# Expert tokens as rows fetched from DRAM, a ring of fourteen weight tiles, and a pad ahead of the last stage's operands

## Chip, cores and metric

One core of one Trainium2 chip. Times are device microseconds (us) of one execution. The kernel is written with a scheduler of tiles: each engine has its own queue of instructions, and the queues meet at semaphores.

## What is computed

The reference runs two blocks over 512 tokens of width 1024. The first ends in a mixture of experts: of 32 experts in 4 groups each token takes the best group and the best two experts in it.

```python
def hierarchical_moe(hn, w_router_group, w_router_expert, w_gate, w_up, w_down):
...
    gates = g_w * jax.nn.softmax(top_v, axis=-1)
...
    xs = tokens[row_token].reshape(n_blocks, EXPERT_BLOCK, d)

    def run_block(args):
        xb, e = args
        return (jax.nn.silu(xb @ w_gate[e]) * (xb @ w_up[e])) @ w_down[e]
...
    out = jnp.zeros((n, d), jnp.float32).at[row_token].add(ys.astype(jnp.float32) * row_gate[:, None])
```

Ahead of it stands a state-space and convolution mixer; behind it a second block with windowed attention, an mLSTM, a merge of their branches and a convolutional feed-forward part. All is float32.

## The kernel before, in words

Tokens are kept as 4 tiles of 128 (NT = 4), the width as 8 tiles of 128 (KD = 8). The program has three stages. phase_a is the mixer, to about 450 us. phase_b has the router (`route`, to about 474 us) and the experts (`experts`, L781, to about 1000 us). phase_c is the second block. Most of its products, as of phase_a's, are at L227: a float32 product as three products of operands that are split in a high and a low part (hT_hi, hT_lo with wh, wl).

**Experts.** Each expert has 64 slots (NSLOT); what does not fit goes through `overflow` (L619), a branch on the count `nov`. The loop runs over 8 groups of 4 experts, each as 2 pairs, 16 pairs in all. For a group, `dispatch` (L743) builds a one-hot matrix S of 512 tokens by 256 slots on DVE, and `gather` (L728) multiplies it with the normalized tokens on PE: 64 matmuls of 128x256 (L738, tile pxg) give the slots' activations transposed, xg. `gather` is a generator; PE works it off piece by piece inside the pairs of the group before. The tokens are split in hn_hi and hn_lo by `route_split` (L441), on ACT, DVE and POOL. A pair has 64 matmuls for gate and up (pgu, L808), an activation, four transposes (phT, L723), and 32 matmuls for down (pyd, L834). `slot_gates` (L753) finds each slot's gate weight and its row in the result (pgs, L763). For the first seven groups (NVIA = 7) POOL scatters the pair's rows to the DRAM buffer y_rows by an indirect DMA (L842); the last group is combined by matmuls (pcomb, L879). `add_rows` (L859) reads y_rows back and adds it to x.

**Weights.** `load_w` (L161) loads tiles of 1 MB in turn into a ring of ten; almost all loads stand in SP's queue, in order, and each waits until the matmuls that read the tile's former content are done. A pair reads twelve tiles: four for gate, four for up, four for down. `expert_loads` (L403) gives their order, with the context products' weights (MK, MV) behind pairs 9 and 12. `prefetch` (L395) takes the next loads from it, `expert_w` one at a time; `phase_b` (L331) calls prefetch(10) once behind `route`, and once on POOL's queue ahead of the overflow's branch, since SP cannot issue loads while it waits at it. `add_rows` issues its eight transfers (L867) on SP's queue as well, between the weights of pairs 13 and 14.

**Places.** Pools are allocated from two sides of the on-chip memory. c_h is opened first in phase_c (L1464) on the right side and holds hT_hi and hT_lo; pools opened on that side later lie below it.

Of the kernel before, what the change touches and what calls it, by code (L numbers as in the profile page):

```python
# [15 lines left out]
I32 = mybir.dt.int32  # L16
# [108 lines left out]
class K:  # L125
# [35 lines left out]
    def load_w(self, src, nk=4, cols=512, rows=False, queue=None):  # L161
        if self.loaded:
            return self.loaded.popleft()
        pool, n = self.rings[self.ring_at % len(self.rings)]
        self.ring_at += 1
        w = pool.tile([P, nk, cols], F32, tag="w", name="w")
        (queue or self.nc.sync).dma_start(w, src if rows else src.rearrange("(k p) c -> p k c", p=P))
        return w
# [77 lines left out]
    def setup(self):  # L246
# [40 lines left out]
        self.ye = self.dram.tile([YROWS, D], F32, name="y_rows")  # L287
        self.mod_at = 0
# [42 lines left out]
    def phase_b(self):  # L331
# [6 lines left out]
        ws = [self.load_w(w[k * P:(k + 4) * P, AK:AK + 512]) for k in (0, 4)]  # L338
        self.route(bp, rt, ws)
        rt.release()  # L340
        wk = self.pool("b_wk", bufs=1)
        i = self.ring_at % 5
        turn = [p for p, _ in self.rings[i:] + self.rings[:i]]
        self.set_rings([(p, 1) for p in (ringm[1], ringm[1], *turn[:3], ringm[2], ringm[2], ringm[0], *turn[3:])])
        self.loads = self.expert_loads({9: MK, 12: MV})
        self.ahead = deque()
        self.prefetch(10)
# [47 lines left out]
    def prefetch(self, n, queue=None):  # L395
        self.ahead.extend(self.load_w(src, rows=True, queue=queue) for src in islice(self.loads, n))

    def expert_w(self):
        if not self.ahead:
# [27 lines left out]
    def route_alloc(self):  # L427
        self.hh = self.bcp.tile([P, NT, KD, P], F32R, tag="s16", name="hn_hi")
        self.hl = self.bcp.tile([P, NT, KD, P], F32R, tag="bcg", name="hn_lo")
# [11 lines left out]
    def route_split(self, t):  # L441

        nc = self.nc
        r = self.xss[:, 0, t:t + 1]
        x = self.x[:, t, :].rearrange("p (h q j) -> p h j q", h=2, j=4)
        h, l = (v[:, t].rearrange("p (h j) q -> p h j q", h=2) for v in (self.hh, self.hl))
        nc.scalar.activation(h, x, AF.Copy, scale=r)
        if t > 1:
            if t == 2:
                self.xr = self.wide.tile([P, 2, D], F32, tag="cva", name="xr")  # L450
            xr = self.xr[:, t - 2, :]
            nc.scalar.activation(xr, self.x[:, t, :], AF.Copy, scale=r)
# [32 lines left out]
    def route_steps(self):  # L485
# [4 lines left out]
        self.route_split(0)  # L490
# [4 lines left out]
        self.route_split(1)  # L495
# [8 lines left out]
    def route(self, bp, rt, ws):  # L504
# [71 lines left out]
        for i, s in enumerate((1, 2, 4, 8, 16)):  # L576
# [7 lines left out]
        self.nov = bp.tile([1, 1], I32, name="nov")  # L584
        nc.vector.tensor_copy(self.nov, src[0:1, E - 1:E])
# [26 lines left out]
        self.gshl = bp.tile([P, NT, E, 3], F32R, name="gshl")  # L612
        tok = self.cst[:, CS["token"]]
        nc.vector.scalar_tensor_tensor(self.gshl[:, :, :, 2], oh2f, float(T),
                                       tok[:, :, None].to_broadcast([P, NT, E]), op0=ALU.mult, op1=ALU.add)
        nc.vector.tensor_copy(self.gshl[:, :, :, 0], gs)
        nc.vector.tensor_sub(self.gshl[:, :, :, 1], gs, self.gshl[:, :, :, 0].bitcast(F32))

    def overflow(self, op, wk):  # L619
# [5 lines left out]
        ei = op.tile([1, 1], I32, name="ei")  # L625
        nov = nc.values_load(self.nov[0:1, 0:1], min_val=0, max_val=2 * T // S)
        with tc.If(nov > 0), tc.For_i(0, nov, 1) as b:
# [37 lines left out]
            for _ in self.gather(xg, Sm, S):  # L665
                pass
# [22 lines left out]
            y = op.tile([S, D], F32, name="oy")  # L689
# [38 lines left out]
    def gather(self, xg, S, n):  # L728

        nc = self.nc  # L730
        g = self.pv[:, PV["norm_ffn4"]]
        for q in range(KD // 2):
            px = self.aux.tile([P, 2, n], F32, tag="ax", name="pxg")
            for kk in range(2):
                k = 2 * q + kk
                for t in range(NT):
                    for j, h in enumerate((self.hh, self.hl)):
                        nc.tensor.matmul(px[:, kk, :], h[:, t, k, :], S[:, t, :],  # L738
                                         start=(t == 0 and j == 0), stop=(t == NT - 1 and j == 1))
            nc.vector.tensor_mul(xg[:, 2 * q:2 * q + 2, :], px, g[:, 2 * q:2 * q + 2, None].to_broadcast([P, 2, n]))  # L740
            yield

    def dispatch(self, S, xg, grp):  # L743
# [7 lines left out]
        return self.gather(xg, S, 4 * NSLOT)  # L751

    def slot_gates(self, wk, S, grp):  # L753

        nc = self.nc
        gs = wk.tile([P, 2], F32, tag="gs", name="gs", bufs=2)
        at = [wk.tile([P, 1], I32, tag=f"at{pr}", name="at", bufs=2) for pr in range(2)]
        for pr in range(2):
            sc = slice(pr * P, pr * P + P)
            pg = self.aux.tile([P, 6], F32, tag="ax", name="pgs")  # L760
            e0 = grp * 4 + pr * 2
            for t in range(NT):
                nc.tensor.matmul(pg, S[:, t, sc],  # L763
                                 self.gshl[:, t, e0:e0 + 2, :].rearrange("p e j -> p (e j)"),
                                 start=(t == 0), stop=(t == NT - 1))
            for i in range(2):
                r = slice(64 * i, 64 * i + 64)
                nc.vector.tensor_reduce(gs[r, pr:pr + 1], pg[r, 3 * i:3 * i + 2], op=ALU.add, axis=AX.X)
                nc.vector.tensor_scalar(at[pr][r, :], pg[r, 3 * i + 2:3 * i + 3], float(NOROW), None, op0=ALU.add)
# [11 lines left out]
    def experts(self, bp, wk, extra):  # L781
# [4 lines left out]
        Ss = [SS[:, i * D:i * D + D].rearrange("p (t c) -> p t c", t=NT) for i in range(2)]  # L786
        xgs = [self.wide.tile([P, KD, 4 * NSLOT], F32, tag=t, name="xg") for t in ("u", "cva")]
        for _ in self.dispatch(Ss[0], xgs[0], 0):
            pass
        back = self.keys  # L790
        for grp in range(8):
            S, xg = Ss[grp % 2], xgs[grp % 2]
            via = grp < NVIA
            if via:
                ahead = self.dispatch(Ss[1 - grp % 2], xgs[1 - grp % 2], grp + 1)
            for pr in range(2):
                e0 = grp * 4 + pr * 2
                pgu = []
                for _ in range(2):
# [16 lines left out]
                if pr == 0:  # L816
                    gs, at = self.slot_gates(wk, S, grp)
                    if not via:
                        ST = Ss[1 - grp % 2].rearrange("p t c -> p (t c)").rearrange("p (r c) -> p r c", r=2)
                        self.take_back(S, ST)  # L820
                        self.add_rows()
                if via:
                    for _ in islice(ahead, 2):
                        pass
# [20 lines left out]
                else:  # L845
                    yhl = self.wide.tile([P, 2, D], F32R, tag="u", name="yhl")
# [7 lines left out]
                if extra[1].get(2 * grp + pr):  # L854
                    extra[1][2 * grp + pr]()
        for _ in back:
            pass

    def add_rows(self):  # L859

        nc = self.nc
        for h, tag in enumerate(("s16", "bcg")):
            r = self.bcp.tile([P, 2, 2, D], F32, tag=tag, name="rows_back")
            for i in range(2):
                t = 2 * h + i
                for k in range(2):
                    nc.sync.dma_start(r[:, i, k, :], self.ye[T * k + P * t:T * k + P * t + P, :])  # L867
                for k in range(2):
                    nc.vector.tensor_add(self.x[:, t, :], self.x[:, t, :], r[:, i, k, :])
# [594 lines left out]
    def phase_c(self):  # L1464
# [5 lines left out]
        lo = ph.tile([P, KD, T], F32R, name="hT_lo")  # L1470
        pt = self.pool("c_tmp", bufs=2)
# [844 lines left out]
```

## Time and profile before

| what | us |
|---|---|
| median of 3 runs | 2036.63 (2034.98 to 2036.65) |
| the profiled execution | 2032.46 |
| its span on the core | 2030.7 |
| PE busy in the span | 1962.0 |
| DVE, ACT, POOL busy | 1027.2, 661.0, 114.1 |
| mean granted clock of PE | 0.993 |
| bytes moved by DMA | 392.86 MB |

The span goes from the first to the last instruction, and the execution's time has some 2 us around it. The clock is a share of full speed. A busy PE is not a PE at its peak: matmuls are pipelined, so a matmul's own duration is longer than the step from one start to the next.

### The profile page before, as it was taken

To read this page: it belongs to the slowest core of one execution; us is meant where nothing else is said; L and a number is where in the kernel's file an instruction comes from. 1 tells how busy PE (TensorE), PEld (TensorE's weight loads), DVE (VectorE), ACT (ScalarE), POOL (GpSimd) and SP (SyncE) were. 2 spreads that over 40 slices of the span, in tenths; PEclk is the share of its full clock that TensorE was granted. 3 is DMA by queue.
4 is the path that set the end of the run, shared out by engine and by line. 5 is a ranking of instruction groups with operands and counts; after the bars stand their busy time and mean duration, and the time that the engine had idled before them with its cause. 6 is when DMAs were issued, how large, how long until landed. Compare 5 with 4: busy or idle time off the path is not lost.

```text
span 2030.7 us, 24234 instructions
## 1 busy us (share of the span) xinstructions
PE 1962.0 (97%) x9533; PEld 1367.5 (67%) x9533; DVE 1027.2 (51%) x1958; ACT 661.0 (33%) x1139; POOL 114.1 (6%) x139
## 2 busy tenths in 40 slices
PE   5999999999999999998999999999999999999999
PEld 5777676785444433443377888778888788888887
DVE  3766758434224111102477687684734666656632
ACT  3332325331010000000256666422433354334411
POOL 2000002000000010000122010000000020000000
PEclk9999999999999999998999999999999999999999
DMA  7344355536999999999832222543133442323231
GB/s 285 129 163 143 112 204 189 181 136 251 420 403 375 421 418 394 422 364 387 343 111 68 63 71 73 173 120 110 58 111 125 135 145 83 104 84 103 96 114 50
DMA packets 121797, 392.86 MB, mean 193 GB/s; under 512 B 12436, under 2 KB 31540, under 8 KB 93008
## 3 DMA queue, kind: packets, MB, share of 16 engines
q1 hardware_dynamic: 110912, 353.63, 47.1%
q0 software_dynamic: 6848, 33.05, 4.1%
q10 hardware_dynamic: 3920, 4.59, 0.7%
q8 instruction: 76, 1.25, 0.3%
q14 instruction: 41, 0.34, 0.1%
HBM read 370.73 MB, written 24.17 MB: 194 GB/s over the span
## 4 chain that ended last, share of the span: by engine, by line
PE 74%; issue 15%; DVE 5%; DMA 4%; ACT 2%; POOL 1%; SPq 0%; POOLq 0%; ACTq 0%; DVEq 0%
PE mm L227 41%; PE pgu L808 10%; PE pyd L834 6%; PE pxg L738 3%; PE pck L1368 2%; DMA w<-in_w_down_dram 2%; PE pav L1737 2%; PE ppt L1724 1%; DMA w<-in_w_up_dram 1%; PE pn L1866 1%; PE pn L1867 1%; DVE wl L132 1%; PE psc L1691 1%; DMA cst<-in_cst_dram 1%; PE pst L1883 1%
## 5 line engine op out<-in xcount | busy, mean ns | idle before, releaser
L132 DVE TENSOR_TENSOR wl<-w,wh 128x1024 fp32r<-128x1024 f32 x206 | 251.5, 1222 | 357.4 <-ACT wh L131 352.3
L131 ACT ACTIVATE wh<-w 128x1024 fp32r<-128x1024 f32 x210 | 222.3, 1059 | 545.4 <-PE mm L227 500.5
L808 PE MATMUL pgu<-w,xg 128*64 128x512 f32 x1024 | 234.9, 597 | 6.0 <-DMA w<-in_w_up_dram 4.6
L227 PE MATMUL mm<-hT_hi,wl 128*128 128x512 f32 (+1 forms) x560 | 219.7, 392 | 0.0
L227 PE MATMUL mm<-hT_lo,wh 128*128 128x512 f32 (+1 forms) x560 | 218.7, 391 | 0.7 <-POOL hT_lo L1312 0.7
L227 PE MATMUL mm<-hT_hi,wh 128*128 128x512 f32 (+1 forms) x560 | 218.7, 391 | 0.0
L808 PEld LDWEIGHTS pgu<-w,xg 128*64 128x64 f32 x1024 | 75.0, 138 | 149.9 <-issue 139.7
L834 PE MATMUL pyd<-w,hT 128*64 128x512 f32 x512 | 143.0, 618 | 9.5 <-DMA w<-in_w_down_dram 7.1
L227 PE MATMUL mm<-hnT_hi,wh 128*128 128x512 f32 (+1 forms) x368 | 144.6, 394 | 0.9 <-DVE rv L137 0.6
L227 PE MATMUL mm<-hnT_lo,wh 128*128 128x512 f32 (+1 forms) x368 | 141.7, 385 | 0.0
L227 PE MATMUL mm<-hnT_hi,wl 128*128 128x512 f32 (+1 forms) x368 | 141.0, 386 | 0.2 <-POOL wl L132 0.2
L227 PEld LDWEIGHTS mm<-hT_lo,wh 128*128 128x128 f32 x560 | 105.3, 188 | 25.5 <-POOL hT_lo L1312 0.9
L227 PEld LDWEIGHTS mm<-hT_hi,wl 128*128 128x128 f32 x560 | 105.3, 188 | 22.9 <-issue 0.4
L227 PEld LDWEIGHTS mm<-hT_hi,wh 128*128 128x128 f32 x560 | 105.3, 188 | 22.2
L834 PEld LDWEIGHTS pyd<-w,hT 128*64 128x64 f32 x512 | 42.5, 140 | 83.4 <-issue 73.6
L227 PE MATMUL mm<-wh,hT_lo 128*128 128x512 f32 (+1 forms) x256 | 95.3, 372 | 1.0 <-DVE hT_lo L1308 1.0
L227 PE MATMUL mm<-wh,hT_hi 128*128 128x512 f32 (+1 forms) x256 | 95.2, 373 | 0.0
L227 PE MATMUL mm<-wl,hT_hi 128*128 128x512 f32 (+1 forms) x256 | 94.7, 372 | 0.0
L227 PEld LDWEIGHTS mm<-hnT_hi,wh 128*128 128x128 f32 x368 | 69.4, 189 | 27.0 <-issue 7.4
L227 PEld LDWEIGHTS mm<-hnT_hi,wl 128*128 128x128 f32 x368 | 69.5, 189 | 16.2 <-issue 1.5
L227 PEld LDWEIGHTS mm<-hnT_lo,wh 128*128 128x128 f32 x368 | 69.5, 189 | 14.3 <-issue 2.1
L714 DVE SCALAR_TENSOR_TENSOR esg<-eth,pgu 128x512 f32<-128x512 f32 x16 | 11.0, 685 | 126.4 <-ACT eth L712 126.4
(552 smaller groups left out, 3468.3 us busy)
## 6 DMA issues: line engine op xcount, KB each, us to landing
w<-in_w_up_dram SPq DMA_DIRECT2D x82, 1024.0 KB, 10.2
w<-in_w_down_dram SPq DMA_DIRECT2D x72, 1024.0 KB, 9.6
w<-in_w_gate_dram SPq DMA_DIRECT2D x60, 1024.0 KB, 7.9
w<-in_w_in_dram SPq DMA_DIRECT2D x56, 1024.0 KB, 6.6
w<-in_w_mod_dram SPq DMA_DIRECT2D x24, 1024.0 KB, 4.8
w<-in_w_out_dram SPq DMA_DIRECT2D x16, 1024.0 KB, 5.2
x_res<-in_x_dram SPq DMA_DIRECT2D x8, 512.0 KB, 8.5
y_rows<-zero_rows POOLq DMA_DIRECT2D x4, 1024.0 KB, 9.2
```

Of the source, the lines that this page charges most:

```text
L131: nc.scalar.activation(hi, src, AF.Copy)
L132: (eng or nc.vector).tensor_sub(lo, src, hi.bitcast(F32))
L227: nc.tensor.matmul(ps[i][:, a:b], x, y, start=st, stop=sp, skip_group_check=(per > 1 or halves))
L738: nc.tensor.matmul(px[:, kk, :], h[:, t, k, :], S[:, t, :], start=(t == 0 and j == 0), stop=(t == NT - 1 and j == 1))
L808: nc.tensor.matmul(ps[64 * i:64 * i + 64, :], xg[:, k, c:c + NSLOT], ws[i][k // 4][:, k % 4, :], start=(k == 0), stop=(k == KD - 1), skip_ ...
L834: nc.tensor.matmul(py[dh][64 * i:64 * i + 64, :], hT[:, f, 64 * i:64 * i + 64], ws[i][:, f % 2 * 2 + dh, :], start=(f == 0), stop=(f == 3) ...
L1368: nc.tensor.matmul(ps[t], self.hc[:, k, t * P:(t + 1) * P], ws[k // 4][:, k % 4, :], start=(k == 0), stop=(k == KD - 1))
L1691: nc.tensor.matmul(pl, u.qs[i], kst[0][:, kv, c0 * P:c0 * P + n], start=True, stop=False)
L1724: nc.tensor.transpose(pt[:, i, :], u.p[i][:, s * P:(s + 1) * P], self.ident)
L1737: nc.tensor.matmul(po[64 * x:64 * x + 64], v[:, vs, kv * 64:kv * 64 + 64], PT[s][:, 2 * x:2 * x + 2, :], start=(s == 0), stop=(s == nk - 1 ...
L1866: nc.tensor.matmul(pn, qs[:, j, cs], C, start=True, stop=False)
L1867: nc.tensor.matmul(pn, Pm[:, j, cs], mv[:, c, h, :], start=False, stop=True)
```

## The change

1. `route_split` is replaced by `route_rows`: ACT scales a tile of tokens and writes it as rows to a DRAM buffer h_rows. `gather` goes. `fetch` reads, by an indirect DMA on POOL, the row of each of a pair's 128 slots; `turn_rows` transposes them on PE (8 transposes of 128x128) into xg. For the offsets the slot matmul gets a fourth column, the token's number, and `slot_gates` becomes a part of `dispatch`. In the overflow's body the same takes the place of the gather.
2. The tiles that held hn_hi and hn_lo become four more weight tiles (ring_s, ring_bcg), and `prefetch(14)` comes ahead of `route`.
3. The read-back of y_rows becomes four loads of 1 MB in the ring, between gate and up of pair 15; `add_rows` only adds, one pair later.
4. A tile of 96 bytes a partition (pad_right) is allocated in c_h behind hT_lo.

```diff
+        more = [self.bcp.tile([P, 2, 4, 512], F32, tag=t, name="ring_" + t) for t in ("s16", "bcg")]
+        self.set_rings([(p, 1) for p in (ringm[1], ringm[1], *turn[:3], ringm[2], ringm[2], ringm[0], *turn[3:])])
+        self.rings[0:0] = [(r[:, i], 0) for r in more for i in range(2)]
+        self.loads = self.expert_loads({9: MK, 12: MV})
+        self.ahead, self.rows_back = deque(), []
+        self.prefetch(14)
         self.route(bp, rt, ws)
...
-            self.prefetch(10, nc.gpsimd)
+            self.prefetch(14, nc.gpsimd)
...
     def prefetch(self, n, queue=None):
-        self.ahead.extend(self.load_w(src, rows=True, queue=queue) for src in islice(self.loads, n))
+        for src in islice(self.loads, n):
+            if type(src) is int:
+
+                w = self.ring_tile().rearrange("p (k a) b -> p k (a b)", k=2)
+                self.nc.sync.dma_start(w, self.ye.rearrange("(k t p) d -> t p k d", k=2, t=NT)[src])
+                self.rows_back.append(w)
+            else:
+                self.ahead.append(self.load_w(src, rows=True, queue=queue))
...
+                if e0 == 30 and src is wu:
+                    yield from range(NT)
...
+    def route_rows(self, t):
+
+        h = self.hrow[:, t % 2, :]
+        self.nc.scalar.activation(h, self.x[:, t, :], AF.Copy, scale=self.xss[:, 0, t:t + 1])
+        self.nc.scalar.dma_start(self.hd[t * P:t * P + P, :], h)
...
+    def fetch(self, rows, at):
+
+        self.nc.gpsimd.indirect_dma_start(
+            out=rows, out_offset=None, in_=self.hd[:, :],
+            in_offset=bass.IndirectOffsetOnAxis(ap=at[:, 0:1], axis=0), bounds_check=T - 1, oob_is_err=False)
+
+    def turn_rows(self, xg, rows, hf, n):
...
+        px = self.aux.tile([P, 4, n], F32, tag="ax", name="pxg")
+        for j in range(4):
+            nc.tensor.transpose(px[:, j, :], src[:, hf, j, :], self.ident[:n, :n])
+        nc.vector.tensor_mul(xg, px, g.to_broadcast([P, 4, n]))
...
+        gs, at = self.dispatch(wk, S, 0)
+        for pr in range(2):
+            self.fetch(rows[:, pr, :], at[pr][:, 1:2])
+        for _ in islice(self.keys, 3):
             pass
+        turn(0)
...
                 if pr == 0:
...
+                    turn(1)
+                    if grp < 7:
+                        gs2, at2 = self.dispatch(wk, S, grp + 1)
+                        for i in range(2):
+                            self.fetch(rows[:, i, :], at2[i][:, 1:2])
+                    else:
                         self.take_back(S, ST)
-                        self.add_rows()
...
+                elif grp < 7:
+                    turn(0)
+                else:
+                    self.add_rows()
...
         lo = ph.tile([P, KD, T], F32R, name="hT_lo")
+        ph.tile([P, 24], F32, name="pad_right")
```

Three places show how the order moves. First SP's queue around the router, where the first loads for the experts stand (w, ring_s and ring_bcg are tiles of the ring; nov is the overflow's count). Before:

```order
L167 DMA w<-in_w_in_dram 128x4x512 x2
L167 DMA w<-in_w_gate_dram 128x2048 x2
L167 DMA w<-in_w_up_dram 128x2048 x2
L167 DMA w<-in_w_gate_dram 128x2048 x2
L167 DMA w<-in_w_up_dram 128x2048 x2
L167 DMA w<-in_w_down_dram 128x2048
L626 TENSOR_LOAD nov
```

Now:

```order
L165 DMA w<-in_w_in_dram 128x4x512 x2
L165 DMA w<-in_w_up_dram 128x2048
L165 DMA ring_bcg<-in_w_gate_dram 128x2048
L165 DMA ring_s_3271<-in_w_gate_dram 128x2048 x2
L165 DMA ring_bcg<-in_w_gate_dram 128x2048
L165 DMA w<-in_w_up_dram 128x2048
L165 DMA w<-in_w_down_dram 128x2048 x2
L165 DMA w<-in_w_up_dram 128x2048 x2
L165 DMA w<-in_w_down_dram 128x2048 x2
L165 DMA w<-in_w_gate_dram 128x2048 x2
L629 TENSOR_LOAD nov
```

Fourteen expert tiles stand ahead of the load of nov where nine stood, and the first gate tiles lie in the four new ones.

Second PE's queue behind the gate and up matmuls of a pair. Before:

```order
L808 MATMUL pgu<-w,xg 64x512 x23
L723 MATMUL phT<-cst,esg 128x128 x4
L738 MATMUL pxg<-SS,hn_hi 128x256
L738 MATMUL pxg<-SS,hn_lo 128x256
L738 MATMUL pxg<-SS,hn_hi 128x256
```

Now:

```order
L824 MATMUL pgu<-w,xg 64x512 x24
L733 MATMUL phT<-cst,esg 128x128 x4
L1438 MATMUL pml<-mr,rsel 128x4 x8
L751 MATMUL pxg<-cst,rows 128x128 x5
L853 MATMUL pyd_4450<-w,hT 64x512
L853 MATMUL pyd_4451<-w,hT 64x512
```

The one-hot products of the next group are gone from between the pair's own matmuls, and the transposes of the next pair's rows stand there.

Third SP's queue at the read-back of y_rows. Before:

```order
L167 DMA w<-in_w_gate_dram 128x2048 x4
L167 DMA w<-in_w_up_dram 128x2048 x4
L867 DMA rows_back<-y_rows 128x1024 x8
L167 DMA w<-in_w_down_dram 128x2048 x4
L167 DMA w<-in_w_gate_dram 128x2048 x4
```

Now:

```order
L165 DMA ring_bcg<-in_w_gate_dram 128x2048 x2
L165 DMA w<-in_w_gate_dram 128x2048 x2
L406 DMA w<-y_rows 128x2x1024 x4
L165 DMA w<-in_w_up_dram 128x2048 x4
L165 DMA ring_s_3271<-in_w_down_dram 128x2048 x2
L165 DMA ring_bcg<-in_w_down_dram 128x2048 x2
```

The read-back stood ahead of pair 14's down weights and stands ahead of pair 15's up weights, in four tiles of the ring.

## Rows read from the trace of the kernel before

**Rows 1.** The page: busy time of each engine (its line).

```profile
PE 1962.0 (97%) x9533; PEld 1367.5 (67%) x9533; DVE 1027.2 (51%) x1958; ACT 661.0 (33%) x1139; POOL 114.1 (6%) x139
```

**Rows 2.** Windows of 40 us across the expert stage, and the sum of its thirteen.

```profile
core 0: us, PE busy (x) PEld busy (x) DVE busy (x) ACT busy (x) POOL busy (x), PEclk, DMA share, GB/s
480.00:520.00 40.00, 39.89 (x194) 17.85 (x192) 8.85 (x26) 4.61 (x11) 3.20 (x3) 1.00 0.92 370
520.00:560.00 40.00, 38.91 (x198) 18.29 (x195) 8.77 (x22) 3.94 (x10) 0.99 (x1) 1.00 1.01 422
...
920.00:960.00 40.00, 31.78 (x140) 11.99 (x138) 13.16 (x20) 3.67 (x6) 0.97 (x1) 0.88 0.95 387
...
sum 520.00, PE 494.56 PEld 211.39 DVE 105.41 ACT 40.76 POOL 23.35; mean PE 38.04 PEld 16.26 DVE 8.11 ACT 3.13 POOL 1.80
```

**Rows 3.** The DMA view of 474:1000, its line of totals.

```profile
DMA packets 33046, 207.47 MB, mean 394 GB/s; under 512 B 4297, under 2 KB 4297, under 8 KB 9594
```

**Rows 4.** Window of everything behind the experts, columns as in rows 2.

```profile
1010.00:2031.00 1021.00, 1006.94 (x4963) 815.18 (x4961) 621.54 (x1174) 440.08 (x806) 60.02 (x83) 1.00 0.31 101
```

**Rows 5.** Timeline of PE in 1700:1703, operand hT: start, duration, instruction.

```profile
1699.80 0.40 PE L227 MATMUL mm<-hT_hi,wl 128*128 128x512 f32 x1
...
1702.84 0.39 PE L227 MATMUL mm<-hT_hi,wh 128*128 128x512 f32 x1
```

**Rows 6.** Timeline of PE in 1365:1368.2, operand attT.

```profile
1365.06 0.62 PE L227 MATMUL mm<-attT,wh 128*128 128x512 f32 x2
...
1367.78 0.62 PE L227 MATMUL mm<-attT,wh 128*128 128x512 f32 x2
```

**Rows 7.** Timeline of PE in 496:498.5: the gather.

```profile
496.10 0.36 PE L738 MATMUL pxg<-SS,hn_hi 128*128 128x256 f32 x1
...
498.44 0.28 PE L738 MATMUL pxg<-SS,hn_lo 128*128 128x256 f32 x1
```

**Rows 8.** Timeline of PE in 989:991: four 128x128 transposes.

```profile
989.15 0.74 PE L723 MATMUL phT<-cst,esg 128*128 128x128 f32 x4 [0.82 <-DVE esg L715]
```

**Rows 9.** Timeline of SP's queue in 405:490, weight loads: first issue, time to the last.

```profile
409.67 12.59 SPq L167 DMA_DIRECT2D w<-in_w_gate_dram  x2
...
448.40 4.31 SPq L167 DMA_DIRECT2D w<-in_w_up_dram  x2
466.37 15.50 SPq L167 DMA_DIRECT2D w<-in_w_down_dram  x4
```

**Rows 10.** Windows of 10 us around the first expert, columns as in rows 2.

```profile
450.00:460.00 10.00, 9.83 (x43) 7.57 (x44) 7.67 (x35) 8.80 (x11) 2.86 (x1) 0.66 1.01 428
...
470.00:480.00 10.00, 10.00 (x64) 6.22 (x64) 2.96 (x5) 0.00 (x0) 0.00 (x0) 1.00 0.16 36
```

**Rows 11.** Timeline of PE in 473:477: the first expert matmuls.

```profile
474.43 2.79 PE L808 MATMUL pgu<-w,xg 128*64 128x512 f32 x12
```

**Rows 12.** Groups of line L842, the scatter on POOL: duration min/median/max.

```profile
L842 POOL DMA_INDIRECT y_rows<-y,at x14: 963/966/1111, 510.2 to 937.1; - x14
...
DMA to landing us min/median/max: 4.0/8.2/10.8
```

**Rows 13.** Waits of SP's queue in 474:1000; us in total, times, longest.

```profile
SPq L867 <- DMA y_rows<-y,at: 8.8, 1, 8.8
```

**Rows 14.** Groups of line L227 by form in 1000:2031; ns min/median/max, first and last start.

```profile
L227 PE MATMUL mm<-hT_hi,wh x560: 276/392/628, 1078.7 to 1901.6; 128*128 128x512 f32 x176, 128*128 128x256 f32 x11
...
L227 PE MATMUL mm<-wh,hT_lo x256: 274/394/586, 1021.0 to 1557.4; 128*128 128x512 f32 x96, 128*128 128x256 f32 x32
...
L227 PE MATMUL mm<-wh,fT_lo x176: 391/397/400, 1902.6 to 2025.6; 128*128 128x512 f32 x176
```

**Rows 15.** Timeline of PE in 956:965: a wait for weights in pair 14.

```profile
957.44 6.84 PE L834 MATMUL pyd<-w,hT 128*64 128x512 f32 x20 [6.59 <-DMA w<-in_w_down_dram]
```

**Rows 16.** The page's costliest groups: the experts' two matmuls; busy us, mean ns.

```profile
L808 PE MATMUL pgu<-w,xg 128*64 128x512 f32 x1024 | 234.9, 597 | 6.0 <-DMA w<-in_w_up_dram 4.6
...
L834 PE MATMUL pyd<-w,hT 128*64 128x512 f32 x512 | 143.0, 618 | 9.5 <-DMA w<-in_w_down_dram 7.1
```

More of the change, by code (lines that the diff above doesn't have):

```diff
@@ L163, in load_w, with ring_tile @@
             return self.loaded.popleft()
+        w = self.ring_tile(nk, cols)
+        (queue or self.nc.sync).dma_start(w, src if rows else src.rearrange("(k p) c -> p k c", p=P))
+        return w
+    def ring_tile(self, nk=4, cols=512):
         pool, n = self.rings[self.ring_at % len(self.rings)]
         self.ring_at += 1
-        w = pool.tile([P, nk, cols], F32, tag="w", name="w")
-        (queue or self.nc.sync).dma_start(w, src if rows else src.rearrange("(k p) c -> p k c", p=P))
-        return w
+        return pool.tile([P, nk, cols], F32, tag="w", name="w") if n else pool
     def pool(self, name, bufs=1, side="right"):
@@ L287, in setup @@
         self.ye = self.dram.tile([YROWS, D], F32, name="y_rows")
+        self.hd = self.dram.tile([T, D], F32, name="h_rows")
         self.mod_at = 0
@@ L341, in phase_b @@
         wk = self.pool("b_wk", bufs=1)
[L342 to L347, printed above, removed]
         gp = self.pool("b_gates")
@@ L395, in prefetch @@
     def prefetch(self, n, queue=None):
-        self.ahead.extend(self.load_w(src, rows=True, queue=queue) for src in islice(self.loads, n))
+        for src in islice(self.loads, n):
[5 more added lines that the diff above has]
+                self.ahead.append(self.load_w(src, rows=True, queue=queue))
     def expert_w(self):
-        if not self.ahead:
+        while not self.ahead:
             self.prefetch(1)
@@ L583, in route @@
         self.ov = ov
-        self.nov = bp.tile([1, 1], I32, name="nov")
-        nc.vector.tensor_copy(self.nov, src[0:1, E - 1:E])
+        self.nov = bp.tile([1, 2], I32, name="nov")
+        nc.vector.tensor_copy(self.nov[:, 0:1], src[0:1, E - 1:E])
         ge = new([NT, 4], "ge")
@@ L610, in route @@
         self.gsel = gs
-        self.gshl = bp.tile([P, NT, E, 3], F32R, name="gshl")
+        self.gshl = bp.tile([P, NT, E, 4], F32R, name="gshl")
         tok = self.cst[:, CS["token"]]
@@ L624, in overflow @@
         wg, wu, wd = a["w_gate"][0], a["w_up"][0], a["w_down"][0]
-        ei = op.tile([1, 1], I32, name="ei")
+        ei = self.nov[:, 1:2]
         nov = nc.values_load(self.nov[0:1, 0:1], min_val=0, max_val=2 * T // S)
@@ L664, in overflow @@
             xg = new([KD, S], "xg")
-            for _ in self.gather(xg, Sm, S):
-                pass
+            y = op.tile([S, D], F32, name="oy")
+            pi = self.aux.tile([P, 4], F32, tag="ax", name="oid")
+            for t in range(NT):
+                nc.tensor.matmul(pi[0:S], Sm[:, t, :], self.gshl[:, t, 0, :], start=(t == 0), stop=(t == NT - 1))
+            rows = op.tile([S, 1], I32, name="orow")
+            nc.vector.tensor_scalar(rows, pi[0:S, 3:4], float(NOROW), None, op0=ALU.add)
+            nc.vector.memset(y, 0.0)
+            self.fetch(y, rows)
+            for hf in range(2):
+                self.turn_rows(xg[:, 4 * hf:4 * hf + 4, :], y, hf, S)
             pgu = []
@@ L726, in ffn_turn, with dispatch @@
         return hT
-    def gather(self, xg, S, n):
-        nc = self.nc
[L731 to L743, printed above, removed]
+    def fetch(self, rows, at):
[3 more added lines that the diff above has]
+    def turn_rows(self, xg, rows, hf, n):
+        nc = self.nc
+        g = self.pv[:, PV["norm_ffn4"]][:, 4 * hf:4 * hf + 4, None]
+        src = rows.rearrange("p (h q j) -> p h j q", h=2, j=4)
+        px = self.aux.tile([P, 4, n], F32, tag="ax", name="pxg")
+        for j in range(4):
+            nc.tensor.transpose(px[:, j, :], src[:, hf, j, :], self.ident[:n, :n])
+        nc.vector.tensor_mul(xg, px, g.to_broadcast([P, 4, n]))
+    def dispatch(self, wk, S, grp):
         nc = self.nc
@@ L750, in dispatch @@
                 self.posm[:, t, grp * 4:grp * 4 + 4, None].to_broadcast([P, 4, NSLOT]), op=ALU.is_equal)
-        return self.gather(xg, S, 4 * NSLOT)
-    def slot_gates(self, wk, S, grp):
-        nc = self.nc
         gs = wk.tile([P, 2], F32, tag="gs", name="gs", bufs=2)
-        at = [wk.tile([P, 1], I32, tag=f"at{pr}", name="at", bufs=2) for pr in range(2)]
+        at = [wk.tile([P, 2], I32, tag=f"at{pr}", name="at", bufs=2) for pr in range(2)]
         for pr in range(2):
-            sc = slice(pr * P, pr * P + P)
-            pg = self.aux.tile([P, 6], F32, tag="ax", name="pgs")
+            pg = self.aux.tile([P, 8], F32, tag="ax", name="pgs")
             e0 = grp * 4 + pr * 2
             for t in range(NT):
-                nc.tensor.matmul(pg, S[:, t, sc],
+                nc.tensor.matmul(pg, S[:, t, pr * P:pr * P + P],
                                  self.gshl[:, t, e0:e0 + 2, :].rearrange("p e j -> p (e j)"),
@@ L785, in experts, with turn @@
         SS = self.wide.tile([P, 2 * D], F32R, tag="cvb", name="SS")
-        Ss = [SS[:, i * D:i * D + D].rearrange("p (t c) -> p t c", t=NT) for i in range(2)]
-        xgs = [self.wide.tile([P, KD, 4 * NSLOT], F32, tag=t, name="xg") for t in ("u", "cva")]
-        for _ in self.dispatch(Ss[0], xgs[0], 0):
+        S = SS[:, 0:D].rearrange("p (t c) -> p t c", t=NT)
+        ST = SS[:, D:2 * D].rearrange("p (r c) -> p r c", r=2)
+        xgs = self.wide.tile([P, 2, KD, P], F32, tag="u", name="xg")
+        rows = self.wide.tile([P, 2, D], F32, tag="cva", name="rows")
+        nc.gpsimd.memset(rows, 0.0)
+        def turn(pr):
+            for hf in range(2):
+                self.turn_rows(xgs[:, pr, 4 * hf:4 * hf + 4, :], rows[:, pr, :], hf, P)
+        gs, at = self.dispatch(wk, S, 0)
+        for pr in range(2):
+            self.fetch(rows[:, pr, :], at[pr][:, 1:2])
+        for _ in islice(self.keys, 3):
             pass
+        turn(0)
         back = self.keys
         for grp in range(8):
-            S, xg = Ss[grp % 2], xgs[grp % 2]
             via = grp < NVIA
-            if via:
-                ahead = self.dispatch(Ss[1 - grp % 2], xgs[1 - grp % 2], grp + 1)
             for pr in range(2):
                 e0 = grp * 4 + pr * 2
+                xg = xgs[:, pr]
                 pgu = []
@@ L855, in experts @@
                     extra[1][2 * grp + pr]()
+            if grp < 7:
+                gs, at = gs2, at2
         for _ in back:
@@ L859, in add_rows @@
     def add_rows(self):
[L861 to L869, printed above, removed]
+        for t, v in enumerate(self.rows_back):
+            for k in range(2):
+                self.nc.vector.tensor_add(self.x[:, t, :], self.x[:, t, :], v[:, k, :])
     def combine(self, ST, yh, yl):
```

45 lines of the change are left out of this document (12 added, 33 removed).

## The prediction

> **What bounds the kernel now.** I read the engines' busy times first, then windows of the experts, then the pace of single matmuls. The first line says TensorE: PE is busy 1962.0 us, 97% of the span, no other engine over 51% [rows 1]. That is an average over stages with different limits, so the expert stage (474 to 1000 us) is read by itself. In its thirteen 40-us windows PE is busy 494.56 of 520 us [rows 2], and so are the transfers: in 520:560 the DMA engines are full (share 1.01) at 422 GB/s, and in 474:1000 they move 207.47 MB [rows 2, 3]. At 422 GB/s that many bytes need 492 us of the 526. So two demands, of about 495 and 492 us, lie beside each other, and where one waits for the other neither makes its full rate: 480:520 has PE full and DMA at 0.92, 920:960 has PE at 31.78 of 40 [rows 2]. A gain here needs both to fall, or the smaller buffer between them to grow.
>
> Behind the experts it is PE alone: 1006.94 of 1021 us busy, granted clock 1.00, DMA at a share of 0.31 [rows 4]. There the pace of the 512-column matmuls counts. With hT as an operand, thirteen steps take 1702.84 - 1699.80 = 3.04 us, 233.8 ns a step [rows 5]. With attT, same line, same clock, twelve steps take 1367.78 - 1365.06 = 2.72 us, 226.7 ns a step [rows 6]. In the built program hT, fT and the other operands of that stage start at an address that is 32 over a multiple of 64 bytes, attT and the split weights at a multiple of 64. That is the one difference I found, and it is a correlation: no row shows the cause.
>
> **The gather leaves PE.** A group's one-hot matmuls (64 of 128x256) go at (498.44 - 496.10)/19 = 0.123 us a step [rows 7]. Seven of the eight groups' lie inside the 520 us: 448 x 0.123 = 55 us less. In come 8 transposes a pair, 15 pairs inside: 120. Four transposes take 0.74 us with the end of the last [rows 8], so at most 0.185 us each (22 us); at least, I say, a gather step each (15 us). I take 18. The slot matmuls (pgs) are as many as before. PE's demand falls to 494.6 - 55 + 18 = 458 us. That by itself gains nothing beyond where DMA sets the end.
>
> **What DMA then has to do.** The fetches move 1024 rows (512 tokens, two experts each) of 4 KB, 4.2 MB; all but the first pair's lie in the stage: +3.9 MB. Four more tiles of 1.05 MB can be resident before the stage starts: -4.2 MB. The read-back is the same 4.2 MB at another place. 207.5 + 3.9 - 4.2 = 207.2 MB, at 422 GB/s 491 us: still more than PE's 458. DMA now sets the stage's end, and its idle time is what can be won.
>
> **The ring and the prefetch.** Before, two tiles are issued at 409.67 to 422, the first ten are only complete with loads of 448 to 466 and later, and then the engines stand still: 36 GB/s in 470:480 [rows 9, 10]. After, SP has fourteen loads ahead of the router's result, the four extra tiles without waiting for the router's operands. They land in time in which the DMA engines are mostly idle, so they cost nothing; if that cover were gone they cost 4.2/0.422 = 10 us. The h_rows write (2.1 MB) goes out on ACT's queue around 450 to 470; in 450:460 the engines are full (428 GB/s [rows 10]), so between 0 and 5 us of delay for weights that nobody reads yet; I take 0.
>
> **The split leaves the router.** Four strided splits on ACT, DVE and POOL go, four plain copies on ACT and their DMAs come. None is a bound there once the gather's operands are no longer wanted; 0, with the cover of the router's own chain.
>
> **The fetch stands in the first pair's path.** Before, the first expert matmul starts at 474.43 [rows 11], right behind the gather. After, it waits for slots, the offsets, a POOL issue and the landing. The nearest row is the scatter, also an indirect DMA of up to 128 rows: 0.97 us on POOL, 8.2 us to landing (4.0 to 10.8) [rows 12]. Slots are complete near 470; 470 + 1 (pgs, offsets) + 1 + 8.2 + 2 (8 transposes and a multiply) gives 482, 8 us later, between 4 and 11. The context keys' matmuls that stood inside pair 0 move into this wait (the new text takes three steps of `keys` ahead of the first transposes), so PE loses little; for DMA, the first ring tile comes free near 484 rather than 478. Later fetches are issued one pair or more ahead of their transposes: with some 30 us a pair the 10 us are covered. What queues behind them on POOL are the scatters, which nobody waits for until the read-back.
>
> **The read-back.** SP waited 8.8 us for the scatter ahead of the eight transfers, with all weight loads behind them in line [rows 13]. After, the same wait is possible at its new place, ahead of pair 15's up weights, but with up to fourteen tiles loaded or in flight. Between 0 and 9 us; I take 4 as idle DMA time. The additions on DVE move to the last pair, beside PE work.
>
> **Sum of the experts.** From 484 on 491 us of transfers: 975, plus the last down matmuls and what idles (4 for the read-back, 3 for the branch at the overflow): 982 instead of 1000, **-18 us**. Ends: -25 if nothing idles; -3 if the ring still runs empty as often as now. Of the rate: 422 GB/s is the trace's own full window. The Trainium skill, DMA: Bandwidth & Descriptors (Specifications), puts the limit of memory to one core at about 358 GB/s, under which 207 MB need 579 us and the stage could not get shorter; the trace has long been above it. Its fabric ceiling of 435 GB/s would make 476 us of the 491, an estimate.
>
> **The places.** c_h's new tile of 96 bytes moves every operand of the later stage to a multiple of 64. The forms [rows 14]: 560 x 176/187 = 527 of 512 columns for hT (three such products), 256 x 96/128 = 192 for hT as moving operand (three), 176 for fT (three): 3 x 895 = 2685, times 7.1 ns = 19 us. PE is 98.6% busy there, so I take **-18**; ends 0 (no row shows that the place is the cause) and -22 (some operands of 64 matmuls each are not in my count).
>
> **Sum.** The profiled execution took 2032.46 us, 4.2 under the median of 2036.63. 2032.5 - 18 - 18 = 1996.5, which stands for 2000.6 in terms of the median: **2000.5 us**.
>
> **Rivals.**
> 1. *The places do nothing.* For: only a correlation over stages that differ otherwise. Against: attT lies in the midst of the same stage, at the same clock [rows 5, 6]. Then only the experts gain: 2036.6 - 18 = 2018.6.
> 2. *The experts give their gain back*, because the ring empties elsewhere (read-back, overflow branch, first fetch). For: the wait of 8.8 [rows 13] and a later start. Against: four more tiles hold 10 us of transfers. Then only the places gain: again 2018.6.
> 3. *Neither*: 2036.
> 4. *Slower: PE starves and its clock falls.* Once DMA sets the pace, PE idles for some 60 us of the stage. After a wait of 6.59 us twenty down matmuls took 6.84 us [rows 15], against 143.0 us busy for 512 of overlapping ones; 920:960 has a granted clock of 0.88, 450:460 has 0.66 [rows 2, 10]. At the lower level, 1.2 instead of 2.4 GHz, expert matmuls cost double; their groups hold 234.9 + 143.0 us of busy time [rows 16]. It decides when PE's 458 grow past DMA's end: each us at the low level adds half a us, so from 2 x (520 - 458) = 124 us at the low level on the stage is slower than now. With 240 us: 458 + 120 = 578 instead of 520, less 18 for the places: 2077. Against: 920:960 had 8.2 us of idle PE, and a mean of 0.88 there is (1 - 0.88)/0.5 x 40 = 9.6 us at the low level [rows 2]; at that ratio the 62 us that PE would idle in the stage bring some 73 us, short of 124. The Trainium skill, TensorE: Matmul & The Clock Gate (HAM oscillation), says that waits for DMA between bursts of matmuls throw the clock back each time; by it, this rival would be the likely one. The trace agrees in the one window of 0.88 and not in the others.
>
> **How the numbers follow.** Chances: forecast 0.62, rival 1 0.14, rival 2 0.14, rival 3 0.05, rival 4 0.05. The forecast's own range is 1990 to 2011 (ends of both terms, not both at once). To hold 8 in 10 the range must take in rivals 1 and 2 with some room: 1987 to 2022. A difference of 0.2%, 4 us, is about what can be told from no change. Faster by more: the forecast and rivals 1 and 2 but for 0.02, plus 0.04 of small gains in 3 and 4's mild form: 0.92. Within: 0.04. Slower: 0.04.
>
> **What would show it.** Right: DMA share at 1.0 in nearly all windows from 490 to the stage's end, that end near 982, PE about 458 + idle; first expert matmul at 478 to 485; hT steps of 227 ns. Wrong: hT steps still at 234 (rival 1); windows with a share under 0.95 or waits of SP over 10 us on the read-back or the branch (rival 2); a granted clock under 0.9 over several windows (rival 4). The forecast fails if the time is over 2022 or under 1987.

## The result, and the profile after

| kernel | median us (range) | ratio to before | profiled span |
|---|---|---|---|
| before | 2036.64 (2034.98 to 2036.93) | | 2030.7 |
| after | 2007.22 (2005.34 to 2007.79) | 0.9856 (0.9839 to 0.9873) | 2006.0 |

29.4 us less; 36 were forecast, within a range of 1987 to 2022. The two profiled spans differ by less, 24.7 us: the profiled execution of before was 4.2 us under its median, that of after 0.6 over its own.

The page's line of busy times after, beside [rows 1]: PE works 65 us less.

```profile
PE 1896.8 (95%) x9149; PEld 1324.1 (66%) x9149; DVE 1020.4 (51%) x1954; ACT 654.8 (33%) x1138; POOL 130.7 (7%) x158
```

Windows of 40 us of after (columns as in [rows 2]), and its DMA totals in 474:990, the answer to [rows 3]:

```profile
480.00:520.00 40.00, 35.46 (x166) 14.17 (x168) 10.03 (x28) 3.20 (x6) 6.71 (x7) 0.90 0.76 303
520.00:560.00 40.00, 38.89 (x183) 15.65 (x179) 9.20 (x24) 4.29 (x10) 3.03 (x3) 1.00 1.01 421
...
720.00:760.00 40.00, 27.20 (x85) 7.89 (x82) 2.10 (x7) 1.88 (x3) 5.36 (x9) 0.91 0.99 412
...
920.00:960.00 40.00, 36.06 (x150) 13.74 (x148) 9.72 (x14) 3.24 (x5) 0.99 (x1) 1.00 1.02 418
960.00:1000.00 40.00, 30.69 (x104) 12.04 (x99) 20.38 (x30) 8.53 (x15) 3.95 (x6) 0.87 0.75 304
sum 520.00, PE 463.20 PEld 179.87 DVE 115.87 ACT 45.70 POOL 44.82; mean PE 35.63 PEld 13.84 DVE 8.91 ACT 3.52 POOL 3.45
```

```profile
DMA packets 34505, 207.27 MB, mean 402 GB/s; under 512 B 5472, under 2 KB 5488, under 8 KB 11694
```

Where DMA had a share of 0.89 to 1.02 from window to window, it has now 0.98 to 1.02 in all eleven from 520 to 960, at 412 to 422 GB/s but for one (388 in 760:800). PE idles instead: 463 us busy where there were 495, and 9.7 of the 463 lie behind the experts (990:1000); 720:760 has 27.20 of 40. The two windows at the ends are the exception: 0.76 at the start; in the last one the experts are over. The last down matmul ends at 989.8 us (986.14 + 3.65, shown below); before, at 999.8:

```profile
990.64 9.14 PE L834 MATMUL pyd<-w,hT 128*64 128x512 f32 x32 [0.75 <-ACT hT L725]
```

So 10 of the 24.7 us come by then, and 14.7 behind it.

Timeline of PE of after with hT as operand, against [rows 5]: thirteen steps in 2.94 us, 226 ns a step instead of 233.8. Below it two forms of the line, against [rows 14]:

```profile
1699.66 0.39 PE L230 MATMUL mm<-hT_hi,wl 128*128 128x512 f32 x1
...
1702.60 0.39 PE L230 MATMUL mm<-hT_hi,wh 128*128 128x512 f32 x1
```

```profile
L230 PE MATMUL mm<-hT_hi,wh x560: 278/389/632, 1071.0 to 1880.8; 128*128 128x512 f32 x176, 128*128 128x256 f32 x11
...
L230 PE MATMUL mm<-wh,fT_lo x176: 389/389/389, 1881.7 to 2000.7; 128*128 128x512 f32 x176
```

The fT products start 20.9 us earlier than before (1881.7 for 1902.6) and end 24.9 earlier (2000.7 for 2025.6): the lead grows along with the matmuls.

The start of the experts on PE, the answer to [rows 11]:

```profile
476.33 1.84 PE L769 MATMUL pgs<-gshl,SS 128*128 128x8 f32 x8 [9.47 <-DVE SS L760]
483.85 2.16 PE L751 MATMUL pxg<-cst,rows 128*128 128x128 f32 x9 [5.68 <-DMA rows<-h_rows,at]
485.94 4.77 PE L824 MATMUL pgu<-ring_s,xg 128*64 128x512 f32 x16
```

The first expert matmul comes at 485.94, 11.5 us later than before. What it waits for is seen on DVE, ACT and SP, in this order:

```profile
467.12 0.17 DVE L592 TENSOR_REDUCE gw<-ge 128x4 f32<-128x16 f32 x1 [5.80 <-ACT ge L590]
...
475.75 1.77 DVE L760 TENSOR_TENSOR SS<-cst,posm 128x256 fp32r<-128x256 f32 x5 [3.80 <-DMA h_rows<-h_out]
```

```profile
452.82 2.18 ACT L458 ACTIVATE h_out<-x_res,x_squares 128x1024 f32<-128x1024 f32 x2
...
464.42 1.15 ACT L458 ACTIVATE h_out<-x_res,x_squares 128x1024 f32<-128x1024 f32 x1 [8.41 <-DMA h_rows<-h_out]
```

```profile
460.02 8.05 SPq L165 DMA_DIRECT2D w<-in_w_gate_dram  x2
490.74 0.81 SPq L165 DMA_DIRECT2D ring_s<-in_w_gate_dram  x2
```

The one-hot tile SS waits for a write to h_rows, since it lies in the buffer that h_out had. ACT's third copy into h_out waits 8.41 us for the write of the first, and the router's exponential (ge), next in ACT's queue, waits with it, and DVE with that (5.80). These writes of 0.5 MB take 10.4 us from issue to landing, while the DMA engines are full (1.02 in 450:460) with the six weight tiles that go out in the same 20 us; how fast they would be without the tiles was not tried. Only at 490.74, when the first pair has read its first tiles, can SP load again.

The tail of pair 15: PE waits for up weights, behind the read-back, and runs the rest at a lower clock (0.87 in 960:1000):

```profile
957.21 3.65 PE L824 MATMUL pgu<-w,xg 128*64 128x512 f32 x16
967.61 1.97 PE L824 MATMUL pgu<-w,xg 128*64 128x512 f32 x2 [6.74 <-DMA w<-in_w_up_dram]
970.34 10.04 PE L824 MATMUL pgu<-w,xg 128*64 128x512 f32 x30 [0.76 <-DMA w<-in_w_up_dram]
...
982.65 3.66 PE L853 MATMUL pyd<-ring_s,hT 128*64 128x512 f32 x16 [0.75 <-ACT hT L735]
986.14 3.65 PE L853 MATMUL pyd<-ring_bcg,hT 128*64 128x512 f32 x16
```

### The profile page after: what moved, and what is told of

The parts are those of the page before. It is cut to its first block, busy times and chain, and to the rows that moved or that the text cites. A ratio compares the mean times of both kernels' runs of the same rounds, so it can differ in the third digit from the quotient of the medians.

```text
span 2006.0 us, 23527 instructions
## 1 busy us (share of the span) xinstructions
PE 1896.8 (95%) x9149; PEld 1324.1 (66%) x9149; DVE 1020.4 (51%) x1954; ACT 654.8 (33%) x1138; POOL 130.7 (7%) x158
## 4 chain that ended last, share of the span: by engine, by line
PE 63%; issue 16%; DMA 13%; DVE 4%; ACT 2%; POOL 1%; SPq 0%; POOLq 0%; ACTq 0%; DVEq 0%
PE mm L230 41%; PE pgu L824 6%; DMA w<-in_w_up_dram 4%; PE pyd L853 3%; DMA w<-in_w_gate_dram 2%; PE pav L1753 2%; PE ppt L1740 2%; DMA w<-in_w_down_dram 1%; DMA ring_s<-in_w_down_dram 1%; DMA ring_bcg<-in_w_down_dram 1%; DMA h_rows<-h_out 1%; DVE wl L132 1%; PE pn L1882 1%; PE pck L1383 1%; PE pxg L751 1%
## 5 line engine op out<-in xcount | busy, mean ns | idle before, releaser
L824 PE MATMUL pgu<-w,xg 128*64 128x512 f32 x736 | 179.3, 615 | 22.7 <-DMA w<-in_w_up_dram 16.8
L824 PEld LDWEIGHTS pgu<-w,xg 128*64 128x64 f32 x736 | 57.3, 141 | 137.8 <-issue 104.9
L853 PE MATMUL pyd<-w,hT 128*64 128x512 f32 x320 | 85.6, 610 | 8.0 <-SPq L630 4.7
L230 PE MATMUL mm<-wh,fT_hi 128*128 128x512 f32 x176 | 68.5, 389 | 0.0
```

The source lines that it names most:

```text
L230: nc.tensor.matmul(ps[i][:, a:b], x, y, start=st, stop=sp, skip_group_check=(per > 1 or halves))
L824: nc.tensor.matmul(ps[64 * i:64 * i + 64, :], xg[:, k, c:c + NSLOT], ws[i][k // 4][:, k % 4, :], start=(k == 0), stop=(k == KD - 1), skip_ ...
L853: nc.tensor.matmul(py[dh][64 * i:64 * i + 64, :], hT[:, f, 64 * i:64 * i + 64], ws[i][:, f % 2 * 2 + dh, :], start=(f == 0), stop=(f == 3) ...
```

## The experiments

Kernels of one group ran on one chip, and before beside them; after was measured apart, so a difference from it goes across chips (before's medians on them lie between 2036.02 and 2037.08). The texts of expectation stand as they were written.

**The places.** Four kernels: the change without the pad, and the kernel before with a pad of 96, 64 or 32 bytes.

```diff
         lo = ph.tile([P, KD, T], F32R, name="hT_lo")
-        ph.tile([P, 24], F32, name="pad_right")
```

```diff
         lo = ph.tile([P, KD, T], F32R, name="hT_lo")
+        ph.tile([P, 24], F32, name="pad_right")
```

(16 and 8 in place of 24 for 64 and 32 bytes.)

> The change without its 96-byte tile: operands of the last stage again 32 bytes over a multiple of 64, all of the experts' part kept. Theory (the place sets the pace): hT steps of 234 ns again, the last stage some 15 us longer than in the change, about 2022 us, 14 to 15 under the kernel before. Rival (the place is nothing, the gain behind the experts came with other parts of the change): about 2007.

> The kernel before with the 96-byte tile alone. Theory: hT steps of 227 ns, the expert stage as before (last down matmul near 1000 us), the last stage 15 us shorter: about 2021 us. Rival: 2036.

> The kernel before with a tile of 64 bytes, so that the operands move but stay 32 bytes over a multiple of 64. Theory (it is the remainder to 64 that counts): no gain, 2036, hT steps of 234 ns. Rival (any move does it, by some collision of two operands' places): about 2021.

> The kernel before with a tile of 32 bytes: the operands stand at a multiple of 64, but 64 over a multiple of 128. Theory (64 is what counts): 2021, steps of 227 ns. Rival (128 is what counts): 2036, steps of 234 or between.

The starts of the operands (hT, fT and the others of that stage) are those of the built programs; no trace shows an address.

| kernel | operands' start in bytes, modulo 128 | median us | ratio to before |
|---|---|---|---|
| pad_undone | 96 | 2025.69 | 0.9949 (0.9932 to 0.9966) |
| pad96_alone | 0 | 2019.56 | 0.9917 (0.9900 to 0.9933) |
| pad64_alone | 32 | 2035.01 | 0.9992 (0.9982 to 1.0002) |
| pad32_alone | 64 | 2028.22 | 0.9962 (0.9949 to 0.9974) |

The place does it: 17.3 us with the pad alone, 18.5 us lost without it, and moving by 64 bytes gives nothing that can be told. But not by a multiple of 64, as I had it: 32 bytes bring about half, 8.7 us (5.3 to 10.4 by the interval). In the timelines of pad32_alone, first fT as the loaded operand (128 columns, second name), then hT as the streamed one (512 columns, first name):

```profile
1949.71 0.40 PE L227 MATMUL mm<-wh,fT_hi 128*128 128x512 f32 x1
...
1951.81 0.39 PE L227 MATMUL mm<-wh,fT_hi 128*128 128x512 f32 x1
```

```profile
1700.09 0.39 PE L227 MATMUL mm<-hT_hi,wh 128*128 128x512 f32 x1
...
1702.83 0.39 PE L227 MATMUL mm<-hT_hi,wh 128*128 128x512 f32 x1
```

Nine steps in 2.10 us are 233 ns, as slow as before; twelve in 2.74 us are 228. At 64 over a multiple of 128 the streamed operand is nearly cured, the loaded one not at all. The same two of pad96_alone:

```profile
1949.79 0.39 PE L227 MATMUL mm<-wh,fT_lo 128*128 128x512 f32 x1
...
1951.83 0.39 PE L227 MATMUL mm<-wh,fT_lo 128*128 128x512 f32 x1
```

```profile
1700.01 0.39 PE L227 MATMUL mm<-hT_hi,wh 128*128 128x512 f32 x1
...
1702.73 0.39 PE L227 MATMUL mm<-hT_hi,wh 128*128 128x512 f32 x1
```

Nine steps in 2.04 us and twelve in 2.72: both go at 227. And hT of pad64_alone, then of pad_undone:

```profile
1700.29 0.40 PE L227 MATMUL mm<-hT_hi,wh 128*128 128x512 f32 x1
...
1703.09 0.40 PE L227 MATMUL mm<-hT_hi,wh 128*128 128x512 f32 x1
```

```profile
1699.68 0.39 PE L230 MATMUL mm<-hT_hi,wh 128*128 128x512 f32 x1
...
1703.18 0.39 PE L230 MATMUL mm<-hT_hi,wh 128*128 128x512 f32 x1
```

Twelve steps in 2.80 us and fifteen in 3.50, 233 both. In the built programs all fast operands, attT and the split weights among them, start at a multiple of 128.

**The ring.**

```diff
-        self.rings[0:0] = [(r[:, i], 0) for r in more for i in range(2)]
-        self.prefetch(14)
+        self.prefetch(10)
...
-            self.prefetch(14, nc.gpsimd)
+            self.prefetch(10, nc.gpsimd)
```

> The change without the four extra weight tiles: a ring of ten, ten loads ahead. Theory (the stage is bound by DMA, and the four tiles bring 4.2 MB ahead of it, 10 us, and fill its gaps): 10 to 20 us slower than the change, 2017 to 2027, with windows of a DMA share under 0.95. Rival (the gather's leaving alone brings the gain): within 4 us of the change.

2018.47 us, 0.9905 (0.9888 to 0.9921): 11.3 us slower than after, and 1.1 under pad96_alone, which has the old gather and the same places. So with ten tiles fetching in place of gathering, with the moved read-back, is worth nothing that can be told, and the four tiles bring the experts' gain. That nothing is a net value: the late start of after is in this kernel too (first expert matmul at 485.83), and the next experiments put its price at some 7 us. A ring of ten without the late start was not run, and the four tiles have their place only because the gather's operands are gone. One expectation hardly held: behind the start, one window is under 0.95. Three windows, and the DMA totals of 474:1002:

```profile
520.00:560.00 40.00, 35.14 (x162) 14.08 (x159) 8.43 (x22) 3.33 (x7) 3.30 (x3) 1.00 1.01 420
...
760.00:800.00 40.00, 32.96 (x134) 12.90 (x133) 4.84 (x7) 2.57 (x4) 3.56 (x5) 0.96 0.92 360
...
880.00:920.00 40.00, 39.13 (x148) 15.28 (x150) 3.51 (x5) 3.08 (x5) 1.01 (x1) 1.00 1.02 416
```

```profile
DMA packets 35190, 210.63 MB, mean 399 GB/s; under 512 B 5544, under 2 KB 5575, under 8 KB 11867
```

Elsewhere DMA is as full with ten tiles (0.89 in 880:920 was before's). The four tiles fill hardly any gap; they bring 4.2 MB ahead of the stage. The totals differ by 210.63 - 207.27 = 3.4 MB up to the experts' end, which comes 12 us later (1002.0): 8 us of transfers at 421 GB/s, and another 3 for 760:800, where after moved 388 GB/s.

**The start.** A tile of its own for tokens 2 and 3 of h_out; then also the buffers of SS and xg exchanged.

```diff
+        if t == 2:
+            self.hrow = self.wide.tile([P, 2, D], F32, tag="cva", name="h_out2")
         h = self.hrow[:, t % 2, :]
```

> The change, with tokens 2 and 3 of h_out in a tile of their own, so that ACT need not wait for the writes of tiles 0 and 1 and the one-hot tile only waits for the first two. Theory (DMA sets the end of the experts, so its start sets it too): first expert matmul at 476 to 479 instead of 485.9, and the end of the experts earlier by the same 7 to 10 us: about 1998 us. Rival (the tail or the overflow branch sets the end): start as above, but under 3 us in the time, 2005 to 2007.

2003.32 us, 0.9830 (0.9813 to 0.9846): 3.9 under after, at the edge of what can be told, where 9 were expected. The start was expected at 476 to 479 and came at 482.34: ACT is free, and SS still waits (DVE, then PE):

```profile
468.22 0.43 DVE L762 TENSOR_TENSOR SS<-cst,posm 128x256 fp32r<-128x256 f32 x1 [8.66 <-DMA h_rows<-h_out]
```

```profile
482.34 1.97 PE L826 MATMUL pgu<-ring_s,xg 128*64 128x512 f32 x4 [0.30 <-DVE xg L754]
```

The end of the experts moved by 2.9 us (to 986.9) with 3.6 of the start. The theory held, its size did not, so the remaining wait was taken out:

```diff
-        SS = self.wide.tile([P, 2 * D], F32R, tag="cvb", name="SS")
+        SS = self.wide.tile([P, 2 * D], F32R, tag="u", name="SS")
-        xgs = self.wide.tile([P, 2, KD, P], F32, tag="u", name="xg")
+        xgs = self.wide.tile([P, 2, KD, P], F32, tag="cvb", name="xg")
```

> The kernel of rows_out_apart with the tiles of the one-hot matrix and of xg exchanged, so that the one-hot matrix no longer waits for a write to h_rows. What held it in rows_out_apart: 8.66 us of DVE's wait on that write. Theory (the start of the experts sets their end): first expert matmul at 476 to 479 instead of 482.3, the end earlier by the same 3 to 6 us, 1997 to 2000 us. Rival (another wait, on the writes' landing by the fetch itself, takes its place): first expert matmul at 480 or later, 2001 to 2004.

1999.94 us, 0.9820 (0.9807 to 0.9834), 7.3 under after and the fastest here; the first expert matmul comes at 479.12, for 476 to 479. PE's start, SP's next load, then the last down matmuls:

```profile
477.24 1.95 PE L753 MATMUL pxg<-cst,rows 128*128 128x128 f32 x8 [10.13 <-DMA rows<-h_rows,at]
479.12 4.28 PE L826 MATMUL pgu<-ring_s,xg 128*64 128x512 f32 x16
```

```profile
483.43 0.81 SPq L165 DMA_DIRECT2D ring_s<-in_w_gate_dram  x2
```

```profile
974.86 3.66 PE L855 MATMUL pyd<-ring_s,hT 128*64 128x512 f32 x16 [0.75 <-ACT hT L737]
978.35 3.65 PE L855 MATMUL pyd<-ring_bcg,hT 128*64 128x512 f32 x16
```

The start is 6.8 us earlier than after's, SP's next load 7.3, the down matmuls 7.8 (974.86 for 982.65). The wait that is left is for the last write to h_rows, which the fetch needs in any case. But on POOL something stands between the two:

```profile
470.61 1.80 POOL L798 MEMSET rows<- 128x2048 f32 x1 [115.51 <-DMA h_rows<-h_out]
472.70 1.14 POOL L742 DMA_INDIRECT rows<-h_rows,at  x1 [0.29 <-DMA w<-in_w_gate_dram]
```

The tile that the fetch fills, rows, is cleared first. In after that is done at 435.5; here rows lies in the buffer that h_out2 was given, so its 1.80 us come behind the last write. Taking them out was not tried.

**The read-back.** First between up and down, its additions behind the transposes; then, on slots_apart, behind down, its additions behind the last combination.

```diff
-                if e0 == 30 and src is wu:
-                    yield from range(NT)
...
+            if e0 == 30:
+                yield from range(NT)
             for f in range(2):
...
-                else:
-                    self.add_rows()
                 hT = self.ffn_turn(wk, sg, P)
+                if pr and not via:
+                    self.prefetch(NT)
+                    self.add_rows()
```

> The change with the read-back between up and down of pair 15, and its additions behind that pair's transposes. Theory (the last weights land at the same time, but the up weights 10 us earlier, so that pair 15's gate and up are done when the down weights land): PE's wait of 6.7 us in pair 15 goes or shrinks, the end 3 to 6 us earlier, 2001 to 2004. Rival (the additions come to stand between the last pair and the norm behind it): 2007 or slower.

2006.85 us, 0.9853 (0.9837 to 0.9870): no difference from after that can be told, where 3 to 6 us were expected. The theory fails: the wait did not shrink, it moved from the up to the down weights:

```profile
976.95 6.32 PE L854 MATMUL pyd<-ring_s,hT 128*64 128x512 f32 x14 [8.53 <-DMA ring_s<-in_w_down_dram]
```

```diff
-                if e0 == 30 and src is wu:
-                    yield from range(NT)
...
+            if e0 == 30:
+                yield from range(NT)
             if e0 // 2 in ctx:
...
-                else:
-                    self.add_rows()
...
+        self.prefetch(NT)
         for _ in back:
             pass
+        self.add_rows()
```

> The kernel of slots_apart with the read-back behind pair 15's down weights and its additions behind the last combination. Theory (the experts' last weights land 10 us earlier, since 4.2 MB come behind them, and the additions, 8 of about 1 us on DVE, run beside the context's matmuls): 3 to 8 us under slots_apart. Rival (the norms wait for the read-back and the additions instead, so that the last stage starts no earlier): within 2 us of slots_apart, or slower by the additions' 8 us.

2001.15 us, 0.9832 (0.9818 to 0.9845): within 2 us of slots_apart. The rival holds, the theory does not:

```profile
963.91 8.65 PE L853 MATMUL pyd<-w,hT 128*64 128x512 f32 x32 [0.75 <-ACT hT L737]
...
973.26 4.13 PE L896 MATMUL pcomb<-yhl,SS 128*128 128x512 f32 x15 [0.28 <-DVE yhl L870]
981.77 14.82 PE L1385 MATMUL pck<-w,hcT 128*128 128x512 f32 x28 [4.38 <-DMA w<-in_w_in_dram]
...
1002.53 0.50 PE L230 MATMUL mm<-wh,hT_hi 128*128 128x512 f32 x1
```

The down matmuls start 11 us earlier than in slots_apart, but then PE waits 4.38 us for the first w_in tile, which now stands behind the read-back, and the last stage's first product (mm) comes at 1002.53, in slots_apart at 1001.69. Whatever comes last in the queue, the bytes ahead of the next stage are the same.

## Why the prediction was right, and where not

- **PE and DMA beside each other; DMA sets the end once the gather is gone: right.** DMA has a share of 0.98 to 1.02 in the eleven windows from 520 to 960; PE is busy 463 us, 453.5 of them up to 990, for a forecast 458. That the gather's leaving alone gains nothing agrees with ring_of_ten (1.1 us), with the late start in it.
- **The sum of the experts, -18: too large.** The medians of the pairs that differ by it alone give -11.2 (pad_undone against before) and -12.3 (after against pad96_alone), the trace -10 (against an execution of before in which the experts ended at 999.8; in that of pad96_alone, with the same experts, they ended at 1002.7). The mis-sized term is the start, "From 484 on": DMA was free to load from 490.7 on. From there to the end 499 us passed, where 498 were forecast, and that is in part luck: the sum names the last down matmuls but adds only the 4 and the 3 to 975. They took 7.1 us (982.65 to 989.8), and the 4 of the read-back did not show. Rival 2 came true in part, since it had named the first fetch among the ways to give the gain back.
- **Why the start was late: the write of h_rows.** I took 0 for it, as "delay for weights that nobody reads yet". Not the weights waited but the buffer: h_out is used twice over, ACT stands until the first write has landed, the router's exponential stands behind it, and the one-hot tile gets the same buffer. The one-hot tile is complete near 477, for slots near 470, and only a landing in 4.3 us, for 8.2, keeps the first matmul at 485.94, for 482. That makes 3.9 of the 6.7 us. The other 2.8 are the first gate tiles: from the first matmul to SP's next load 4.8 us passed, where the forecast took 2. With both of h_out's waits taken away SP loads again at 483.43, the experts end at 982.0, the forecast 982, and the time is 1999.94, the forecast 2000.5. That it is so near is luck in part: the first matmul is 2.9 us earlier than forecast and the next load comes 4.3 behind it.
- **The places, -18: right in size** (17.3 and 18.5; rival 1 falls with them), wrong in its rule: a multiple of 128, not of 64. In the 192 products that it lists with hT as the moving operand hT is the loaded one, and in the 527 the streamed one; the count stands.
- **The read-back's cost, 4 us of idle DMA:** none showed, 418 GB/s in 920:960. It costs its bytes and a wait of PE, 6.7 us, that does not matter by itself.
- **Rival 4, the clock:** the granted clock fell where PE waited (0.87 in 960:1000, 0.90 in 480:520). The Trainium skill, TensorE: Matmul & The Clock Gate (HAM oscillation), says that waits for DMA throw the clock back; the trace agrees in these windows (and not in 880:960, at 1.00, where PE waited for weights twice, 1.3 us at the longest). In the middle of the stage its price was hidden, since PE was waiting for weights anyway: 0.91 in 720:760, with DMA at 0.99. At the ends it was not. In pair 15 it took 10.04 us for 30 matmuls instead of some 6.5, at most 3.5 us of the tail. At the start the first sixteen gate matmuls took 4.77 us, for 3.65 of sixteen at full clock (957.21), and the first tile came free some 1.1 us later for it. The window there:

```profile
480.00:490.00 10.00, 6.15 (x23) 3.12 (x25) 3.76 (x10) 0.72 (x2) 3.50 (x4) 0.59 0.19 50
```

What stays open: by the steps the places are worth the forecast's 19 us or more, the medians show 17.3 to 18.5, and the two profiled executions 14.7 behind the experts. Matmul by matmul, after leads before by 9.9 us at 1031 us of before, by 11.0 at 1303 and by 8.8 at 1394: across the attention's part the lead did not grow. What holds that part was not tried.

## To carry to other kernels

Once transfers set the end of a stage, as here, count two things first: the bytes that must come inside it, and the moment at which the first buffer comes free. The buffers filled ahead of this stage were worth little more than their bytes (ring_of_ten), and a late start was passed on about in full (2.9 us for 3.6, 7.8 for 6.8), so what a new DRAM round trip holds up through shared buffers and in-order queues has to be followed to the first consumer. And where TensorE is the bound, compare the steps of equal matmuls by operand: a difference of 3% can be a place in memory.

## What was not expected of the hardware

- A float32 product's step of 128x512 depends on where its operands start. Mean steps of hT's and fT's products: 226 to 228 ns at a multiple of 128 bytes (after, pad96_alone); 233 to 235 for the loaded operand at 32, 64 or 96 over one (pad64_alone, pad32_alone, before); for the streamed operand 227 to 231 at 64, 233 at 32, 231 to 236 at 96. Why is not shown.
- Writes of 0.5 MB on ACT's queue, beside six weight tiles on SP's, took 10.4 us to land in after, with the DMA engines at a share of 1.02 in 450:460.
